# A float32 decoder trunk on one core: twelve instead of eight row tiles of each down projection as seven products, and more low parts of the mixers' weights made by transfers

## The chip, the core and the metric

The kernel runs on one core of a Trainium2 chip. Its time is the device time of one execution in microseconds (us), the median of several runs; lower is better. Four engines of the core work side by side, each through its own queue in order: PE (TensorE, matrix products), DVE (VectorE), ACT (ScalarE) and POOL (GpSimd, which here only issues transfers). SP issues the other transfers. Engines wait for one another by semaphores.

## The reference

Two layers; in each, a first feed-forward half step, a mixer (a gated recurrence beside windowed attention, joined through sigmoid gates) and a second feed-forward half step, each between two RMS norms. x is 512 tokens by 1024, all in float32. What the change touches:

```python
def swiglu(h, w_gate, w_up, w_down):              # D_MODEL = 1024, D_FF = 2816 = 22 * 128
    return (jax.nn.silu(h @ w_gate) * (h @ w_up)) @ w_down
...
    x = x + 0.5 * rms_norm(swiglu(h, w_ffn1_gate[l], w_ffn1_up[l], w_ffn1_down[l]), gn[1])
...
    mixed = jax.nn.sigmoid(gate_a) * y_hg + jax.nn.sigmoid(gate_b) * y_at
    x = x + rms_norm(mixed @ w_out[l], gn[3])
...
    x = x + 0.5 * rms_norm(swiglu(h, w_ffn2_gate[l], w_ffn2_up[l], w_ffn2_down[l]), gn[5])
```

The gates gate_a and gate_b are columns of h @ w_in[l]; y_hg and y_at are the two branches after their own projections.

## The kernel before

**Three matmuls for one.** A float32 operand is split into a high part (rounded to the fast matmul format) and the rest, its low part. `mm3` adds high x high, high x low and low x high, so one product of tiles is three matmuls. Of a weight tile, ACT makes the high part `whi` (a cast) and DVE the low part `wlo` (a subtraction). For tiles of kind v, a and d the low part is made otherwise: ACT writes the negated weights, rounded, to `wlo` (`scalar.mul(it.lo, w, -1.0)`), and a transfer issued by POOL adds the raw weights onto them (`accum_op=ALU.add`), so that the difference is left. Activations are split in the same way by ACT and DVE (both are called `s` in the profile, and every accumulator in PSUM is called `acc`).

**The weights' stream.** The class `Stream` (`ws`) loads all weights in order through SP: raw tiles `w` of 128x1024 into 5 buffers (`W32`), each freed when its last reader is done. `split` turns a raw tile, or a sum of raw tiles built by DVE in a buffer `tt` (of which there are 2), into a piece of `whi` and `wlo` in 6 buffers (`WS`). `ws.lead` says how many pieces are prepared ahead: 3, and 5 within a down projection. A piece's buffers come free when PE has used the piece six places earlier.

**Seven products.** A 2x2 block product takes seven products of quarter size instead of eight if sums and differences of the quarters are formed first (numbered 1 to 7 here, as in `operand`). The gate and up projections and a part of the mixers' gates are done so (`sevenths`, 256-column matmuls). Of a down projection, the row tiles in `SEVEN = (7, 11)`, counted in pairs, are: 8 of 22. Token halves and halves of the row tiles are the quarters of the activations, row halves and column halves (h = 0, 1) those of the weights.

**A down projection before** (`Down.seven`; four of them, two in each layer). Seven plain pieces for columns h = 0 (24 matmuls each, into four accumulators, one for each 128 tokens), then the seven products, each as two pieces of 12 matmuls in a row: 1, 5, 6, 2, 7, 4, 3. Then seven plain pieces for h = 1. Products 1, 6, 7 and 3 add up in the same two accumulators (token tiles 0 and 1), and `keep` has ACT copy them to SBUF between two products, because the other quarters need the partial sums: the copy after product 1 is s1, that after 6 is s2, that after 7 is s3. Product 6 adds onto the accumulators that s1 is copied from, so its first matmul waits for the copy. `sums`, `lower` and `differences` build the activations' operands: each takes DVE instructions of 256 columns, an ACT cast and a DVE subtraction of 512.

**The order of the work.** PE's order is the order in which the code is written, with `order.poll()` letting side work in. The other engines' queues are filled by a scheduler from the same program; on each of them an instruction that waits holds up all that stands behind it.

**The mixers.** `LATE = 6` of the 8 column tiles of the attention gate are plain projections (`branch`), the others, and all eight of the other gate, go in pairs as seven products (`branches`).

Of the kernel before, what the change touches and what calls it, by code (L numbers as in the profile page):

```python
# [7 lines left out]
F32 = mybir.dt.float32  # L8
# [3 lines left out]
ALU = mybir.AluOpType  # L12
# [3 lines left out]
P = 128  # L16
# [13 lines left out]
SLOTS = 59  # L30
SEVEN, LAST = (7, 11), 4
BANKS, RESERVE = 8, 2
# [9 lines left out]
def trunk(ctx: ExitStack, tc: tile.TileContext, xin, wall, gains, lbT, hgain, sinks, c_dist, c_mask, c_ident, out):  # L42
# [162 lines left out]
    class Item:  # L205


        def __init__(self, kind, u, left=8):
            self.kind, self.u, self.left = kind, u, left

    class Stream:
# [58 lines left out]
        def rows(self, kt, order=None):  # L270

            u0, r0 = self.n, self.n - self.off
            at = {p: i for i, p in enumerate(order or [(j, h) for j in range(kt // 2) for h in range(2)])}
            for j in range(kt // 2):
                for h in range(2):
                    b = [(4 * h + i) * kt + 2 * j for i in range(4)]
                    if kt == 8:
                        c = b[0] % 8 * P
                        self.src[u0 + at[j, h]] = [(None, wall[r0 + 4 * h : r0 + 4 * h + 4, :, c : c + 2 * P].rearrange("u p c -> p u c"))]
                    else:  # L280
                        self.src[u0 + at[j, h]] = [
                            (slice(i * 2 * P, (i + 1) * 2 * P), wall[r0 + n // 8][:, n % 8 * P : (n % 8 + 2) * P])
                            for i, n in enumerate(b)
                        ]
            if not order:
                self.plain(kt)

        def downs(self):

            a, b = SEVEN  # L290
            rest = [j for j in range(FT // 2) if not a <= j < b]
            m = (b - a) // 2
            up, low = range(a, a + m), range(a + m, b)
            first = [(j, 0) for j in rest]
            seven = [(j, h) for js, h in ((up, 0), (up, 1), (low, 1), (low, 0)) for j in js]
            self.rows(FT, first + seven + [(j, 1) for j in rest])
            self.plain(3, "v")
            self.plain(len(rest) - 3)
            u = self.n
            for kind, q in (("1", 0), ("5", 1), ("6", 2), ("7", 2), ("2", 3), ("4", 3), ("3", 2)):  # L300
                self.items += [Item(kind, u + m * q + i) for i in range(m)]
            self.n += 4 * m
            self.plain(len(rest))

# [18 lines left out]

        def sevens(self, it):

            u, m = it.u, (SEVEN[1] - SEVEN[0]) // 2
            w = self.raw[u]
            if it.kind == "5":
                t = self.tt[u] = sb.tile([P, D], F32, tag="tt", name=nm("tt"), bufs=2)
                vector.tensor_tensor(t, w, self.raw[u - m], op=ALU.subtract)  # L330
                self.release(u - m)
                return t
            if it.kind == "6":
                t = self.tt[u - m]
                vector.tensor_tensor(t, w, t, op=ALU.subtract)
                return t
            if it.kind == "7":
                t = self.raw[u - m]
                vector.tensor_tensor(t, w, t, op=ALU.subtract)
                return t  # L340
            if it.kind == "4":
                t = self.tt.pop(u - 2 * m)
                vector.tensor_tensor(t, w, t, op=ALU.subtract)
                return t
            return w

        def split(self):
            it = self.items[self.done]
            u, last = it.u, it.kind in "uvd"
            self.load(u + (1 if it.kind in "uv1234567" else 2))  # L350
            it.hi = sb.tile([P, D], F32R, tag="whi", name=nm("whi"), bufs=WS)
# [13 lines left out]
            elif it.kind == "c":  # L365

                t = sb.tile([P, D], F32, tag="tt", name=nm("tt"), bufs=2)
                vector.tensor_tensor(t[:, h[0]], self.t13[:, h[0]], v[:, h[1]], op=ALU.add)
                vector.tensor_tensor(t[:, h[1]], t[:, h[0]], w[:, h[1]], op=ALU.add)
                w = t  # L370
            elif it.kind == "d":
                w = v
                cols = h[1:]
            elif it.kind in "1234567":
                w = self.sevens(it)
# [10 lines left out]
            self.flight += 1  # L386
            m = (SEVEN[1] - SEVEN[0]) // 2
            if last:
                self.release(*range(u, u + (1 if it.kind in "uv" else 2)))
            elif it.kind == "7":  # L390
                self.release(u - m)
            elif it.kind in "43":
                self.release(u)

# [239 lines left out]
    class Down:  # L634
# [3 lines left out]
        def __init__(self, src, l, n, nxt):  # L638
# [5 lines left out]
            self.ss = [small([P, 2], "ss2", 8) for _ in range(TT)]  # L644
            self.left = TT

        def gain(self):
# [35 lines left out]
        def post(self, t):  # L683
            for h in range(2):
                if self.yg[t][h] is None:
                    self.square(t, h, self.y[t][h])
                    self.scaled(t, h, self.y[t][h])
            rc = self.root(self.ss[t])
# [120 lines left out]

        def product(self, n, bs, t0, h, start, stop):  # L810

            for u, b in enumerate(bs):
                for t in range(2):
                    for i in range(2):
                        st = cut(self.operand(n, 2 * u + i), slice(t * P, (t + 1) * P))
                        mv = [w.rearrange("p (m two c) -> p m two c", two=2, c=P)[:, :, i, :] for w in b[2:]]
                        mm3(self.y[t0 + t][h], st, mv, start and u == i == 0, stop and (u, i) == (len(bs) - 1, 1), True)
                        order.poll()
                    ws.used(b)

        def seven(self):
# [7 lines left out]
            for t in range(TT):  # L829
                y[t][0] = acc()  # L830
            work = [lambda q=q: self.raws(q) for q in range(m)] + [lambda p=p: self.sums(p) for p in range(2 * m)]
            work += [lambda p=p: self.lower(p) for p in range(m)]
            ws.lead = 5
            for n, j in enumerate(js):
                self.ready(ks[: 4 * n + 4 + EARLY])
                for w in work[2 * n - 2 : 2 * n] if n else ():
                    w()
                b = ws.next(8, TT)
                for t in range(TT):
                    for i in range(2):  # L840
                        self.piece(b, t, 0, j, i, n == i == 0, False, True)
                    ws.used(b)
                    order.poll()
            for t in range(TT):
                y[t][1] = acc()

            def take(n):
                return [ws.next(8, 2) for _ in range(n)]

# [5 lines left out]

            self.product(1, take(m), 0, 1, True, True)
            s1 = keep(0)
            for p in range(m):
                self.differences(p)
            self.product(5, take(m), 2, 1, True, True)  # L860
            s5 = keep(2)
            for p in range(m, 2 * m):
                self.differences(p)
            self.product(6, take(m), 0, 1, False, True)
            s2 = keep(0)
            b7 = take(m)
            self.product(2, take(m), 0, 0, False, True)
            for t in range(2):
                vector.tensor_tensor(s5[t], s5[t], s2[t], op=ALU.add)
            self.product(7, b7, 0, 1, False, True)  # L870
            s3 = keep(0)
            for t in range(2):
                vector.tensor_copy(y[t][1], s5[t])
                vector.tensor_tensor(y[2 + t][1], y[2 + t][1], s3[t], op=ALU.add)
            self.product(4, take(m), 2, 0, False, True)
            self.gain()
            self.product(3, take(m), 0, 1, False, False)
            self.residual()
# [6 lines left out]
            for j in js[: len(js) - LAST]:  # L885
                b = ws.next(8, TT)
                for t in (2, 3, 0, 1):
                    for i in range(2):
# [657 lines left out]
```

## Time and profile before

| | |
|---|---|
| median of three runs | 2093.43 us (2093.42 to 2093.84) |
| the profiled execution | 2094.18 us, span 2092.4 us, granted TensorE clock 0.999 |
| PE busy | 2085.2 us, 100% of the span, 13129 matmuls |
| DVE busy | 1583.7 us, 76% |
| ACT busy | 1191.5 us, 57% |
| DMA | 313.67 MB, mean 150 GB/s |
| low parts by transfer | 188 (105 of 512 KB, 83 of 256 KB) |

Busy times of different engines overlap. In the profile `L169` is the line of every matmul and `L162` that of every DVE and ACT instruction, so instructions are told apart by the names of their tiles. A start that is given as "D0 + n" below counts from the first matmul of a down projection.

### The profile page before, as it was taken

How to read it: one execution, taken by the hardware profiler on the slowest of the kernel's cores; microseconds unless marked ns; L12 is line 12 of the kernel's file. 1: busy time of each engine (PE TensorE's matmuls, PEld its weight loads, DVE VectorE, ACT ScalarE, POOL GpSimd, SP SyncE). 2: the span in 40 equal slices, each digit the busy share in tenths (PEclk: the TensorE clock that was granted, in tenths of full speed). 3: DMA queues.
4: the chain of work that ended last, by engine and by line, in shares of the span. 5: the costliest groups of instructions: out<-in, count | busy, mean ns of one | idle time of the engine just before them, and what ended most of it. 6: DMA issues, size and time to landing. Idle time of an engine off the chain costs nothing.

```text
span 2092.4 us, 34536 instructions
## 1 busy us (share of the span) xinstructions
PE 2085.2 (100%) x13129; PEld 1879.9 (90%) x13129; DVE 1583.7 (76%) x2768; ACT 1191.5 (57%) x1906; POOL 162.1 (8%) x192
## 2 busy tenths in 40 slices
PE   9999999999999999999999999999999999999999
PEld 7999988888898899998889998898788988999987
DVE  6987785777875688878488877758888748888693
ACT  7666655455554656665566665644565546566652
POOL 0111100000010011110001110000000000111100
PEclk9999999999999999999999999999999999999999
DMA  8588734222156758783666776532121666577732
GB/s 250 144 205 191 187 121 166 98 74 72 31 152 196 186 142 189 186 200 105 199 170 177 180 189 167 175 117 91 62 70 54 169 191 182 154 186 180 196 126 66
DMA packets 150918, 313.67 MB, mean 150 GB/s; under 512 B 16128, under 2 KB 73952, under 8 KB 150752
## 3 DMA queue, kind: packets, MB, share of 16 engines
q1 hardware_dynamic: 123536, 234.60, 34.0%
q0 software_dynamic: 27072, 76.82, 20.8%
q8 instruction: 103, 1.69, 0.3%
q14 instruction: 63, 0.52, 0.1%
q10 hardware_dynamic: 144, 0.05, 0.0%
HBM read 219.87 MB, written 14.73 MB: 112 GB/s over the span
## 4 chain that ended last, share of the span: by engine, by line
PE 99%; DMA 0%; DVE 0%; ACT 0%; SPq 0%; issue 0%
PE acc L169 97%; PE acc L177 2%; DMA s<-xin 0%; DVE wlo L162 0%; ACT whi L162 0%; DVE s L162 0%; ACT s L162 0%; SPq L314 0%; SPq L1398 0%; SPq L185 0%; DVE rt L162 0%
## 5 line engine op out<-in xcount | busy, mean ns | idle before, releaser
L169 PE MATMUL acc<-s,whi 128*128 128x256 f32 (+1 forms) x6152 | 1275.7, 306 | 0.0
L169 PEld LDWEIGHTS acc<-s,whi 128*128 128x128 f32 x6152 | 996.7, 191 | 47.9 <-issue 0.5
L169 PE MATMUL acc<-s,wlo 128*128 128x256 f32 (+1 forms) x3076 | 937.5, 305 | 0.6 <-DVE wlo L162 0.5
L169 PEld LDWEIGHTS acc<-s,wlo 128*128 128x128 f32 x3076 | 587.7, 191 | 26.5 <-DVE wlo L162 1.4
L169 PE MATMUL acc<-whi,s 128*128 128x512 f32 x1856 | 582.0, 391 | 0.0
L162 ACT CAST whi<-w 128x1024 fp32r<-128x1024 f32 (+1 forms) x373 | 354.5, 953 | 317.5 <-PE acc L169 174.4
L169 PEld LDWEIGHTS acc<-whi,s 128*128 128x128 f32 x1856 | 348.5, 188 | 75.1 <-issue 3.2
L169 PE MATMUL acc<-wlo,s 128*128 128x512 f32 x928 | 361.3, 389 | 0.0
L162 DVE TENSOR_TENSOR wlo<-w,whi 128x1024 fp32r<-128x1024 f32 (+1 forms) x185 | 223.9, 1215 | 117.2 <-ACT whi L162 107.5
L382 POOL DMA_DIRECT2D wlo<-w x188 | 161.9, 861 | 1802.3 <-ACT wlo L162 826.5
L162 ACT CAST whi<-tt 128x1024 fp32r<-128x1024 f32 x190 | 199.4, 1049 | 162.1 <-DVE tt L162 138.3
L162 DVE TENSOR_TENSOR s<-s,s 128x256 f32<-128x256 f32 (+4 forms) x481 | 246.8, 542 | 19.0 <-ACT s L162 15.8
L162 DVE TENSOR_TENSOR wlo<-tt,whi 128x1024 fp32r<-128x1024 f32 x190 | 231.9, 1220 | 17.7 <-ACT whi L162 15.7
L169 PEld LDWEIGHTS acc<-wlo,s 128*128 128x128 f32 x928 | 174.3, 188 | 34.9
L162 DVE TENSOR_TENSOR m<-acc,s 128x512 f32<-128x512 f32 (+1 forms) x249 | 145.1, 587 | 68.3 <-PE acc L169 65.2
L162 ACT ACTIVATE wlo<-w 128x1024 fp32r<-128x1024 f32 (+1 forms) x188 | 163.2, 868 | 18.3 <-PE acc L169 17.9
L162 ACT CAST s<-s 128x512 fp32r<-128x512 f32 (+1 forms) x180 | 97.1, 586 | 112.8 <-DVE s L162 112.7
L162 DVE TENSOR_TENSOR tt<-tt,w 128x512 f32<-128x512 f32 x166 | 114.6, 690 | 4.6
L162 ACT COPY s<-acc 128x512 f32<-128x512 f32 (+2 forms) x181 | 85.4, 484 | 54.1 <-PE acc L177 28.9
L162 ACT ACTIVATE s<-acc 128x512 f32<-128x512 f32 (+1 forms) x101 | 58.5, 600 | 68.3 <-PE acc L169 67.7
L162 DVE SCALAR_TENSOR_TENSOR s<-m 128x512 f32<-128x512 f32 x73 | 50.4, 691 | 50.7 <-ACT m L162 50.7
L162 ACT ACTIVATE s<-s 128x512 f32<-128x512 f32 (+1 forms) x86 | 53.7, 630 | 51.3 <-DVE s L162 51.2
(95 smaller groups left out, 1225.5 us busy)
## 6 DMA issues: line engine op xcount, KB each, us to landing
w<-wall SPq DMA_DIRECT2D x275, 512.0 KB, 3.9
wlo<-w POOLq DMA_DIRECT2D x105, 512.0 KB, 5.7
w<-wall SPq DMA_DIRECT2D x352, 128.0 KB, 2.9
wlo<-w POOLq DMA_DIRECT2D x83, 256.0 KB, 3.9
x_d<-s SPq DMA_DIRECT2D x48, 256.0 KB, 2.2
s<-x_d SPq DMA_DIRECT2D x48, 256.0 KB, 5.1
w<-wall SPq DMA_DIRECT2D x42, 256.0 KB, 3.1
grow<-rows_d SPq DMA_DIRECT2D x6, 512.0 KB, 4.3
```

The source lines that it names most:

```text
L162: return f(*a, **kw)
L169: nc.tensor.matmul(o, lhsT, rhs, start=start, stop=stop, skip_group_check=loose)
L177: nc.tensor.transpose(o, src, ident)
L382: nc.gpsimd.dma_start(it.lo[:, c].bitcast(F32), w[:, c], accum_op=ALU.add)
```

## The change

Down projections: `SEVEN` becomes (5, 11), so twelve row tiles (three groups of two upper and two lower tiles, called units here) go by seven products, and ten are plain. The order of the work is rewritten: four plain pieces for h = 0, the three pieces of product 1, then for each unit one piece each of products 5, 6, 4 and 2, then the three pieces of product 7, the fifth plain piece (`MID`), the three of product 3 and the plain pieces of h = 1. For a unit's sums of weights only one `tt` buffer is used, in place: raw tile minus raw tile gives 5, a third raw tile minus that gives 6, a fourth minus that gives 4. The raw tiles for 7 and 3 are loaded a second time, nine tiles more in each down projection. Kind "tv" (the plain pieces 0 to 2, the pieces of products 1 and 2) has its low part made by a transfer. The sum s5 + s2 is no longer written back into an accumulator but added in `post` (`also`).

Mixers: `LATE` becomes 4, so one more pair of gate tiles goes by seven products, and the low parts of 14 pieces of each mixer are made by transfers instead of by DVE.

```diff
-SEVEN, LAST = (7, 11), 4
+SEVEN, LAST, MID = (5, 11), 4, 1
-W32, WS, AHEAD, TAIL, PLAIN, FIRST, EARLY, LATE = 5, 6, 3, 2, 3, 6, 4, 6
+W32, WS, AHEAD, TAIL, PLAIN, FIRST, EARLY, LATE = 5, 6, 3, 2, 3, 6, 4, 4
...
+            def five(c, u):
+                c[0] = sb.tile([P, D], F32, tag="tt", name=nm("tt"), bufs=2)
+                sub(c[0], raw[u + 1], raw[u])
+                return c[0]
+
+            def onto(c, u):
+                sub(c[0], raw[u], c[0])
+                return c[0]
...
+            plain(min(3, len(front)), "tv")
+            plain(len(front) - 3, "t")
+            plain(m, "tv")
+            for _ in range(m):
+                u, c = self.n, [None]
+                item("t", u + 1, lambda c=c, u=u: five(c, u), (u, u + 1))
+                item("t", u + 2, lambda c=c, u=u: onto(c, u + 2), (u + 2,))
+                item("t", u + 3, lambda c=c, u=u: onto(c, u + 3))
+                item("tv", u + 3, lambda u=u: raw[u + 3], (u + 3,))
+                self.n += 4
...
-                if it.kind in "vad":
+                if it.kind in ("v", "a", "d", "tv"):
...
+            for u in range(m):
+                self.unit(1, u, 0, 1, True)
             s1 = keep(0)
...
+            for u in range(m):
+                for f, v in work[2 + 2 * u : 4 + 2 * u]:
+                    pair(f, v)
+                self.unit(5, u, 2, 1, True)
+                if u == m - 1:
+                    s5 = keep(2)
+                self.unit(6, u, 0, 1, False)
+                if u == m - 1:
+                    s2 = keep(0)
+                self.unit(4, u, 2, 0, False)
+                self.unit(2, u, 0, 0, False)
...
-                ws.plain(2 * H + 6 + 8 + LATE * 3 // 2)
+                ws.plain(2 * H + 6)
+                ws.plain(8 + LATE * 3 // 2, "v")
```

Three places of the first down projection, in the engines' own orders. The order is the same in the other three. First PE, where product 5 ends (accumulators 3248 and 3249 before, 3146 and 3147 now) and product 6 begins; before, with two pieces of product 5 between product 1 and here:

```order
L169 MATMUL acc_3249<-whi_3177,s_3106 128x512
L169 MATMUL acc_3249<-wlo_3178,s_3106 128x512
L169 MATMUL acc_3249<-whi_3177,s_3107 128x512
L169 MATMUL acc_3246<-whi_3212,s_3057 128x512
L169 MATMUL acc_3246<-wlo_3213,s_3057 128x512
```

And now:

```order
L169 MATMUL acc_3147<-whi_3043,s_3069 128x512
L169 MATMUL acc_3147<-wlo_3044,s_3069 128x512
L169 MATMUL acc_3147<-whi_3043,s_3070 128x512
L169 MATMUL acc_3144<-whi_3097,s_3062 128x512
L169 MATMUL acc_3144<-wlo_3098,s_3062 128x512
```

Product 6 of unit 0 now starts on product 1's accumulators (3144, 3145) one piece of 12 matmuls after product 1 has ended, where it was two pieces.

Second ACT, around the copies of product 1's accumulators (s1). Before:

```order
L162 CAST whi_3212<-tt_3136 128x1024
L162 CAST whi_3241<-tt_3179 128x1024
L162 CAST whi_3262<-w_523_2943 128x1024
L162 COPY s_3294<-acc_3246 128x512
L162 CAST whi_3284<-w_526_2952 128x1024
L162 COPY s_3295<-acc_3247 128x512
```

Now (s_3158 is the high part of the fourth sum of activations, which belongs to unit 1; s_3162 and s_3166 are parts for unit 1 too):

```order
L162 ACTIVATE wlo_3183<-w_526_2954 128x1024
L162 CAST whi_3182<-w_526_2954 128x1024
L162 CAST s_3158<-s_3155 128x512
L162 CAST s_3162<-s_2492 128x512
L162 CAST whi_3204<-tt_3206 128x1024
L162 CAST s_3166<-s_2625 128x512
L162 COPY s_3242<-acc_3144 128x512
L162 COPY s_3243<-acc_3145 128x512
```

The copies now stand behind four casts for unit 1, the first of which reads a sum that DVE makes.

Third DVE, where its work on the down projection begins, before:

```order
L162 SCALAR_TENSOR_TENSOR s_2912<-m_2761 128x512
L162 TENSOR_TENSOR s_2924<-s_646,s_2923 128x512
L162 TENSOR_TENSOR s_2928<-s_780,s_2927 128x512
L162 TENSOR_TENSOR s_2932<-s_917,s_2931 128x512
L162 TENSOR_TENSOR s_2936<-s_1052,s_2935 128x512
L162 TENSOR_TENSOR tt_3136<-w_523_2943,w_500_2861 128x1024
```

Now:

```order
L162 SCALAR_TENSOR_TENSOR s_2912<-m_2761 128x512
L162 TENSOR_TENSOR s_2924<-s_646,s_2923 128x512
L162 TENSOR_TENSOR s_2928<-s_780,s_2927 128x512
L162 TENSOR_TENSOR s_2932<-s_917,s_2931 128x512
L162 TENSOR_TENSOR tt_3045<-w_503_2884,w_500_2861 128x1024
L162 TENSOR_TENSOR s_2936<-s_1052,s_2935 128x512
```

The first subtraction of raw tiles (`tt`) stands one row earlier and reads raw tiles 7 and 8 of the down projection (w_500, w_503) instead of 7 and 9. From it to the instruction that completes s_3155, DVE's order now holds 35 instructions.

More of the change, by code (lines that the diff above doesn't have):

```diff
@@ L293, in downs @@
             up, low = range(a, a + m), range(a + m, b)
[L294 to L301, printed above, removed]
@@ L808, in operand, with unit @@
             return cut((self.x24 if n in (2, 4) else self.x37)[p], HALF[n in (3, 4)])
[L810 to L819, printed above, removed]
+        def unit(self, n, u, t0, h, start):
+            b = ws.next(8, 2)
+            for t in range(2):
+                for i in range(2):
+                    st = cut(self.operand(n, 2 * u + i), slice(t * P, (t + 1) * P))
+                    mv = [w.rearrange("p (m two c) -> p m two c", two=2, c=P)[:, :, i, :] for w in b[2:]]
+                    mm3(self.y[t0 + t][h], st, mv, start and u == i == 0, False, True)
+                    order.poll()
+                ws.used(b)
         def seven(self):
@@ L886, in seven @@
                 b = ws.next(8, TT)
-                for t in (2, 3, 0, 1):
+                for t in range(TT):
                     for i in range(2):
```

137 lines of the change are left out of this document (76 added, 61 removed).

## Prediction

> **What bounds the kernel now.** I read the busy times first, then the chain that ended last, then the stretches of one down projection.
>
> ```profile
> PE 2085.2 (100%) x13129; PEld 1879.9 (90%) x13129; DVE 1583.7 (76%) x2768; ACT 1191.5 (57%) x1906; POOL 162.1 (8%) x192
> PE 99%; DMA 0%; DVE 0%; ACT 0%; SPq 0%; issue 0%
> core 0: us, PE busy (x) PEld busy (x) DVE busy (x) ACT busy (x) POOL busy (x), PEclk, DMA share, GB/s
> 239.30:277.40 38.10, 38.10 (x170) 31.56 (x169) 31.27 (x49) 18.40 (x29) 0.00 (x0) 1.00 0.47 139
> 277.40:315.50 38.10, 38.10 (x169) 31.53 (x168) 32.00 (x38) 22.15 (x29) 0.00 (x0) 1.00 0.52 160
> ```
>
> PE is busy for 2085.2 of 2092.4 us, and the chain is PE from end to end. The two stretches are the plain pieces for h = 0 of the first down projection and its seven products: PE never waits there, and DVE has 6 to 7 us of air in each 38. So time can be won only by fewer or shorter matmuls, and lost by any wait of PE, of which there is now next to none.
>
> **What PE saves.** The pitch of matmuls, start to start, from PE's timeline: three matmuls of 512 columns, then three of 256.
>
> ```profile
> 241.16 0.61 PE L169 MATMUL acc<-whi,s 128*128 128x512 f32 x2
> 241.84 0.61 PE L169 MATMUL acc<-whi,s 128*128 128x512 f32 x2
> 238.24 0.40 PE L169 MATMUL acc<-s,whi 128*128 128x256 f32 x2
> 238.60 0.40 PE L169 MATMUL acc<-s,whi 128*128 128x256 f32 x2
> ```
>
> That is 0.68/3 = 0.2267 us and 0.36/3 = 0.12 us each. A down projection had 14 x 24 + 14 x 12 = 504 matmuls of 512 columns and now has 10 x 24 + 21 x 12 = 492: 12 x 0.2267 = 2.72 us, four times 10.88. In each mixer two plain gate tiles (48 matmuls of 512, 10.88 us) become seven products (84 of 256, 10.08 us): 0.80 each, 1.6 together. PE saves 12.5 us if it waits nowhere.
>
> **Where it will wait.** Product 6 of unit 0 needs s1 copied out of its accumulators first. PE reaches it after 4 x 24 + 3 x 12 + 12 = 144 matmuls, at D0 + 144 x 0.2267 = D0 + 32.64 us. ACT does the copies only after four casts, the first of which needs the sum s_3155 from DVE. So I count DVE's order from its first subtraction of raw tiles to s_3155: 8 instructions of 1024 columns, 8 of 512, 19 of 256. Their pitches, where DVE runs through (starts of neighbouring rows):
>
> ```profile
> 246.94 2.49 DVE L162 TENSOR_TENSOR s<-s,s 128x512 fp32r<-128x512 f32 x4
> 252.92 1.23 DVE L162 TENSOR_TENSOR tt<-w,w 128x1024 f32<-128x1024 f32 x1 [3.49 <-DMA w<-wall]
> 254.06 1.22 DVE L162 TENSOR_TENSOR wlo<-w,whi 128x1024 fp32r<-128x1024 f32 x1
> 255.20 0.69 DVE L162 TENSOR_TENSOR s<-s,s 128x512 fp32r<-128x512 f32 x1
> 255.80 1.22 DVE L162 TENSOR_TENSOR tt<-w,w 128x1024 f32<-128x1024 f32 x1
> 278.18 0.41 DVE L162 TENSOR_TENSOR s<-s 128x256 f32<-128x256 f32 x1
> 278.52 1.02 DVE L162 TENSOR_TENSOR s<-s,s 128x512 fp32r<-128x512 f32 x2
> ```
>
> 1.14, 0.60 and 0.34 us: 8 x 1.14 + 8 x 0.60 + 19 x 0.34 = 20.4 us. Then ACT, pitches again:
>
> ```profile
> 227.93 1.05 ACT L162 CAST whi<-w 128x1024 fp32r<-128x1024 f32 x1 [1.73 <-issue]
> 228.88 1.05 ACT L162 ACTIVATE wlo<-w 128x1024 fp32r<-128x1024 f32 x1
> 245.59 2.17 ACT L162 CAST s<-s 128x512 fp32r<-128x512 f32 x4
> 281.76 0.59 ACT L162 COPY s<-acc 128x512 f32<-128x512 f32 x1 [0.32 <-PE acc L169]
> ```
>
> Three casts of 512 columns (2.17/4 = 0.54 each), one of 1024 (0.95) and the copy (0.59): 3.2 us, with 0.1 for the hand-over to PE 3.3. If DVE's subtraction starts at D0 + t, PE waits t + 20.4 + 3.3 - 32.64 = t - 8.9 us. That ACT stands behind a late DVE is nothing strange here:
>
> ```profile
> ACT s L162 <- DVE s L162: 172.1, 94, 9.1
> ```
>
> **What t is.** The subtraction needs raw tile 8. These are PE's first rows of the four down projections (D0), and SP's last of four transfers for raw tile 8 in each, with the time to its landing:
>
> ```profile
> 239.32 0.40 PE L169 MATMUL acc<-whi,s 128*128 128x512 f32 x1
> 932.32 0.40 PE L169 MATMUL acc<-whi,s 128*128 128x512 f32 x1
> 1274.26 0.40 PE L169 MATMUL acc<-whi,s 128*128 128x512 f32 x1
> 1967.25 0.40 PE L169 MATMUL acc<-whi,s 128*128 128x512 f32 x1
> ...
> L311 SPq DMA_DIRECT2D w<-wall x1: 430/430/430, 246.3 to 246.3; - x1
> DMA to landing us min/median/max: 5.1/5.1/5.1
> L311 SPq DMA_DIRECT2D w<-wall x1: 437/437/437, 939.1 to 939.1; - x1
> DMA to landing us min/median/max: 3.8/3.8/3.8
> L311 SPq DMA_DIRECT2D w<-wall x1: 432/432/432, 1281.7 to 1281.7; - x1
> DMA to landing us min/median/max: 3.6/3.6/3.6
> L311 SPq DMA_DIRECT2D w<-wall x1: 430/430/430, 1975.1 to 1975.1; - x1
> DMA to landing us min/median/max: 3.3/3.3/3.3
> ```
>
> Landed at D0 + 12.1, 10.6, 11.0 and 11.1; the waits would be 3.2, 1.7, 2.1 and 2.2 us, 9.2 together. But now the low parts of product 1's pieces are transfers too, and two of them are issued before that landing, when ACT has raw tiles 4 and 5.
>
> ```profile
> q0 software_dynamic: 27072, 76.82, 20.8%
> wlo<-w POOLq DMA_DIRECT2D x105, 512.0 KB, 5.7
> L311 SPq DMA_DIRECT2D w<-wall x1: 1302/1302/1302, 236.4 to 236.4; - x1
> DMA to landing us min/median/max: 7.1/7.1/7.1
> ```
>
> The queue q0 carries these transfers: 20.8% of 2092.4 us is 435 us for 76.8 MB, so 512 KB take about 3 us of all 16 engines. The last two rows show a load of raw tile 5 that lies between two of them: issue held up to 1.3 us, landing after 7.1. Against the 3.3 to 5.1 above that is 2 to 4 us more. Raw tile 9 no longer crowds raw tile 8 (SP now holds its load until the transfer from raw tile 4 is done), which gives back about 1. I take 2 us, with 0 and 4 as ends. The four waits are then 5.2, 3.7, 4.1 and 4.2: 17.2 us.
>
> **The rest of the change.**
> - SP loads nine raw tiles more in each down projection, and loads wait for low-part transfers. Behind the held load of tile 9, tiles 10 to 12 take four issues of 0.43 us each (the rows above), 1.7; tile 12 is needed 9.5 us after the first subtraction by the pitches above. Cost 0; if DVE does catch up with it, the lateness adds to each wait, up to 2 us. POOL's queue holds nothing but such transfers.
> - Product 2 of unit 1 has its low part by transfer, behind an ACT cast that waits for DVE. By the same counting its matmuls would wait 0.6 us less than product 6 did, so they fall into the wait already paid. Products 4 and 2 of unit 2 likewise, by under 1 us. I add nothing; a transfer slower than 5.7 would be paid in full.
> - DVE's load within the products falls (over the kernel 56 subtractions of 1024 columns from raw tiles fewer, 32 on sums of tiles more), but only behind the place where PE waits.
> - The additional sum in `post` (0.60 us of DVE) lies under the next token tile's matmuls, 24 x 0.2267 = 5.4 us.
> - The mixers' 28 additional transfers free DVE of 28 x 1.14 us and cost ACT a pass each. A piece there lasts 5.4 us, three are made ahead, the transfer takes 5.7: hidden. PE's whole idle time before was 2092.4 - 2085.2 = 7.2 us, start and end included, so there is little to win. 0, within 1 us for each mixer.
>
> **Sum.** -10.9 - 1.6 + 17.2 = +4.7 us on the profiled 2094.18 us; that run lies 0.75 above the median of 2093.43, so 2098.2 on the median's scale.
>
> **Rivals.**
> - *DVE keeps ahead of the loads* (faster). If raw tile 8 were no limit, DVE would arrive at the subtraction about D0 + 10: before, its four activation rows (the row at 246.94) ended at D0 + 10.1; one of them now stands behind the subtraction, and a pass more of ACT ahead of them. Each wait is then 1.1 us: -12.5 + 4.4 = -8.1, 2085. Against it speaks that the landings above are all later. It decides below a mean wait of 2.1 us.
> - *The landings stay as they are*: -12.5 + 9.2 = -3.3, 2090. The loads of tile 8 stand ahead of most of the second transfer; the row with 7.1 us speaks against.
> - *The clock falls during the waits.* The only stretch of several us in which PE idles is the end:
>
> ```profile
> 2084.00:2088.00 4.00, 3.64 (x28) 2.97 (x26) 2.67 (x6) 1.56 (x4) 0.00 (x0) 1.00 0.35 101
> 2088.00:2092.40 4.40, 0.01 (x1) 0.00 (x0) 0.06 (x1) 0.38 (x2) 0.00 (x0) 0.71 0.42 119
> ```
>
> The granted clock (third number from the right) is 0.71 there. If matmuls ran at 0.71 after each wait for as long as it lasted, 4.3 x (1/0.71 - 1) = 1.8 us, four times 7: 2105. [...] The row of the end agrees that idling lowers the clock, but nothing here shows whether a wait of 4 us is enough.
>
> **How the numbers follow.** About 0.2% (4.2 us) is what a measurement can tell from no change. Forecast, waits with landings 1 to 4 us later: 2094 to 2106, likeliest 2098, chance 0.42. Landings as before, 2087 to 2094: 0.25. DVE ahead, 2081 to 2087: 0.20. Clock: 0.13, 2102 to 2109. Slower: the clock and 0.32 of the forecast, 0.45. Faster: DVE ahead and 0.07 of the second, 0.27. Within 0.2%: 0.28. The range 2084 to 2106 leaves out some 0.1 at each end.
>
> **What would show it.** PE should show one wait for ACT of 2 to 6 us at D0 + 32.6 in each down projection, ended by the copy `s<-acc`; DVE no idle time from D0 + 13 to there; 12 matmuls less in each down projection at the same pitch; and the page 244 low-part transfers instead of 188. The forecast is wrong if PE's chain is still unbroken there (then DVE had its tile earlier), or if PE waits at products 4 or 2 instead, or in the mixers.

## The result, and the profile after

The changed kernel takes 2119.5 us (median of four runs, 2117.2 to 2122.3) against 2093.6 us (the three runs of before and a fourth, 2094.00): 1.0124 times the time before, 95% interval 1.0112 to 1.0136. The sign was forecast; the size was not (2098.2 us, range to 2106). The profiled run has a span of 2116.7 us against 2092.4, 24.3 us more. The page of the changed kernel, its busy times, queues, chain, one group of matmuls and the low-part transfers:

```profile
PE 2084.8 (98%) x13153; PEld 1880.8 (89%) x13153; DVE 1587.9 (75%) x2808; ACT 1256.2 (59%) x1994; POOL 210.2 (10%) x248
...
q1 hardware_dynamic: 144848, 253.48, 36.1%
q0 software_dynamic: 35136, 105.66, 28.1%
...
PE 86%; DMA 5%; issue 4%; SPq 2%; ACT 1%; DVE 1%; POOL 0%; POOLq 0%; DVEq 0%; ACTq 0%
...
wlo<-w POOLq DMA_DIRECT2D x159, 512.0 KB, 5.6
...
wlo<-w POOLq DMA_DIRECT2D x85, 256.0 KB, 3.8
```

The chain of work that ended last has left PE: 14% of it now runs through transfers, issue, ACT and DVE. The low parts made by transfers are 159 + 85 = 244, as the change says. PE's waits (total, times, longest), and from the timeline the four places (start, duration, and in brackets the idle time before it and who ended it):

```profile
PE acc L169 <- ACT s L162: 25.9, 4, 6.6
```

```profile
277.73 0.80 PE L169 MATMUL acc<-whi,s 128*128 128x512 f32 x1 [6.39 <-ACT s L162]
278.32 0.63 PE L169 MATMUL acc<-wlo,s 128*128 128x512 f32 x1
278.75 1.05 PE L169 MATMUL acc<-whi,s 128*128 128x512 f32 x2
...
977.04 0.80 PE L169 MATMUL acc<-whi,s 128*128 128x512 f32 x1 [6.65 <-ACT s L162]
...
1325.63 0.80 PE L169 MATMUL acc<-whi,s 128*128 128x512 f32 x1 [6.38 <-ACT s L162]
...
2024.36 0.80 PE L169 MATMUL acc<-whi,s 128*128 128x512 f32 x1 [6.51 <-ACT s L162]
```

There is one wait in each down projection, at the first matmul of product 6 of unit 0, ended by ACT. ACT's timeline before the first of them shows the queue in front of the copy:

```profile
274.59 1.14 ACT L162 CAST s<-s 128x512 fp32r<-128x512 f32 x2 [1.70 <-DVE s L162]
275.63 1.04 ACT L162 CAST whi<-tt 128x1024 fp32r<-128x1024 f32 x1
276.58 0.61 ACT L162 CAST s<-s 128x512 fp32r<-128x512 f32 x1
277.10 1.06 ACT L162 COPY s<-acc 128x512 f32<-128x512 f32 x2
```

ACT stood idle until DVE gave it the first of four casts; the copies of product 1's accumulators, which had been ready for over 8 us, came behind them. DVE in turn had started on the units with this subtraction (the rows of the four down projections):

```profile
253.94 1.23 DVE L162 TENSOR_TENSOR tt<-w,w 128x1024 f32<-128x1024 f32 x1 [5.52 <-DMA w<-wall]
...
953.03 1.22 DVE L162 TENSOR_TENSOR tt<-w,w 128x1024 f32<-128x1024 f32 x1 [5.80 <-DMA w<-wall]
...
1301.85 1.23 DVE L162 TENSOR_TENSOR tt<-w,w 128x1024 f32<-128x1024 f32 x1 [4.52 <-DMA w<-wall]
...
2000.48 1.23 DVE L162 TENSOR_TENSOR tt<-w,w 128x1024 f32<-128x1024 f32 x1 [5.08 <-DMA w<-wall]
```

The first matmuls of the four down projections start at 238.48, 936.86, 1286.23 and 1984.78, so DVE began at D0 + 15.5, 16.2, 15.6 and 15.7, each time after waiting about 5 us for the load of raw tile 8. Finally the stretches of the first wait, of the piece behind it and of the next (length, busy us and instructions of each engine, then the granted clock, the DMA engines' share and GB/s):

```profile
271.30:277.70 6.40, 0.03 (x1) 0.00 (x0) 6.39 (x11) 4.70 (x8) 0.86 (x1) 0.85 0.65 136
277.70:282.80 5.10, 5.07 (x12) 4.01 (x13) 5.03 (x9) 2.02 (x3) 0.00 (x0) 0.52 0.87 253
282.80:285.60 2.80, 2.80 (x14) 2.28 (x14) 1.74 (x3) 1.31 (x2) 0.00 (x0) 1.00 0.63 188
```

Behind the wait the granted clock is 0.52, and twelve matmuls take 5.1 us (starts 0.43 us apart in the rows above) instead of 2.7. In the other three down projections they took 5.1 to 5.3 us, and in the fourth two matmuls behind them were slow as well, so that the slow clock cost 2.4, 2.6, 2.4 and 2.9 us. So the sum of the traces is -12.5 (matmuls) + 26.3 (waits in this group, 0.4 of them for DVE) + 10.3 (slow clock) = +24.1, within a microsecond of the 24.3 us.

### The profile page after: what moved, and what is told of

Its sections match the earlier page's. It is cut to its first block, busy times and chain, and to the rows that moved or that the text cites. A ratio compares the mean times of both kernels' runs of the same rounds, so it can differ in the third digit from the quotient of the medians.

```text
span 2116.7 us, 35203 instructions
## 1 busy us (share of the span) xinstructions
PE 2084.8 (98%) x13153; PEld 1880.8 (89%) x13153; DVE 1587.9 (75%) x2808; ACT 1256.2 (59%) x1994; POOL 210.2 (10%) x248
## 3 DMA queue, kind: packets, MB, share of 16 engines
HBM read 238.74 MB, written 14.73 MB: 120 GB/s over the span
## 4 chain that ended last, share of the span: by engine, by line
PE 86%; DMA 5%; issue 4%; SPq 2%; ACT 1%; DVE 1%; POOL 0%; POOLq 0%; DVEq 0%; ACTq 0%
PE acc L169 84%; DMA w<-wall 4%; SPq L356 2%; PE acc L177 2%; DMA wlo<-w 1%; DVE s L162 1%; ACT s L162 1%; DVE tt L162 0%; ACT wlo L162 0%; ACT whi L162 0%; POOL wlo L404 0%; ACT m L162 0%; DVE m L162 0%; POOLq L404 0%; DVEq L162 0%
## 5 line engine op out<-in xcount | busy, mean ns | idle before, releaser
L169 PEld LDWEIGHTS acc<-s,wlo 128*128 128x128 f32 x3100 | 592.4, 191 | 24.3 <-DVE wlo L162 0.3
L169 PE MATMUL acc<-whi,s 128*128 128x512 f32 x1824 | 580.7, 396 | 26.3 <-ACT s L162 25.9
L404 POOL DMA_DIRECT2D wlo<-w x244 | 210.0, 861 | 1837.7 <-ACT wlo L162 1086.4
L162 ACT CAST whi<-tt 128x1024 fp32r<-128x1024 f32 x206 | 216.1, 1049 | 224.3 <-DVE tt L162 203.6
L162 DVE TENSOR_TENSOR s<-s,s 128x256 f32<-128x256 f32 (+4 forms) x521 | 264.9, 538 | 22.3 <-ACT s L162 15.4
L162 DVE TENSOR_TENSOR wlo<-tt,whi 128x1024 fp32r<-128x1024 f32 x206 | 251.5, 1221 | 25.0 <-ACT whi L162 23.0
L162 ACT ACTIVATE wlo<-w 128x1024 fp32r<-128x1024 f32 (+1 forms) x244 | 221.9, 909 | 17.1 <-PE acc L169 16.7
L162 DVE TENSOR_TENSOR wlo<-w,whi 128x1024 fp32r<-128x1024 f32 (+1 forms) x129 | 154.2, 1212 | 60.5 <-ACT whi L162 58.6
L162 ACT CAST s<-s 128x512 fp32r<-128x512 f32 (+1 forms) x196 | 105.2, 579 | 83.6 <-DVE s L162 77.0
L162 ACT COPY s<-acc 128x512 f32<-128x512 f32 (+3 forms) x183 | 84.2, 486 | 30.1 <-PE acc L177 20.4
L162 DVE TENSOR_TENSOR tt<-w,w 128x512 f32<-128x512 f32 (+1 forms) x97 | 72.8, 750 | 21.1 <-DMA w<-wall 20.9
```

The lines of the kernel that those rows point to most:

```text
L162: return f(*a, **kw)
L169: nc.tensor.matmul(o, lhsT, rhs, start=start, stop=stop, skip_group_check=loose)
L404: nc.gpsimd.dma_start(it.lo[:, c].bitcast(F32), w[:, c], accum_op=ALU.add)
```

## The experiments

Each kernel was timed in three rounds or more beside the kernel before on the same chip. Ratios are to it, with 95% intervals.

| run | what it is | us | ratio |
|---|---|---|---|
| fill | changed + PE kept busy in the wait | 2116.8 | 1.0111 (1.0096 to 1.0126) |
| no_wait | changed, copy s1 not waited for | 2122.1 | 1.0134 (1.0119 to 1.0149) |
| m1_dve | changed, product 1's low parts by DVE | 2106.7 | 1.0065 (1.0049 to 1.0082) |
| mid_early | changed, fifth plain piece ahead of the units | 2139.3 | 1.0217 (1.0202 to 1.0233) |
| down_only | changed down projections alone | 2124.3 | 1.0145 (1.0129 to 1.0160) |
| mix_only | changed mixers alone | 2091.7 | 0.9991 (0.9981 to 1.0000) |
| both | m1_dve and mid_early | 2127.7 | 1.0165 (1.0148 to 1.0182) |
| trio | both, a piece moved behind product 7 | 2128.2 | 1.0163 (1.0148 to 1.0178) |
| m1_w6 | m1_dve, six raw buffers | 2117.3 | 1.0114 (1.0099 to 1.0129) |
| after_w6 | changed, six raw buffers | 2122.0 | 1.0137 (1.0121 to 1.0152) |
| both_w6 | both, six raw buffers | 2107.2 | 1.0064 (1.0049 to 1.0079) |
| mix2 | mix_only, one pair more | 2106.1 | 1.0059 (1.0042 to 1.0076) |
| m1_w6_nw | m1_w6, copy s1 not waited for | 2100.9 | 1.0037 (1.0024 to 1.0050) |
| both_w6_dve | both_w6, product 2's low parts by DVE | 2099.3 | 1.0027 (1.0017 to 1.0037) |

**fill: is it idleness that slows the matmuls?**

```diff
+                if u == 0:
+                    t = order.t
+                    for _ in range(14):
+                        mm(y[2][0][:, :P], zeros, ones, False, False, True)
+                    order.t = t
                 self.unit(6, u, 0, 1, False)
```

> The changed kernel, with 14 matmuls by a tile of zeros (128 columns each, some 0.45 us) put on PE in each down projection between product 5 and product 6 of unit 0, so that PE works through the wait for the copy instead of standing idle. The work of ACT, DVE and the queues is the same. My theory: the slow matmuls after the wait (pitch 0.427 us instead of 0.2267, granted clock 0.50) come from the idleness alone. Then the clock stays at 1.00 and product 6 takes 2.7 us instead of 5.1: 2.4 us less in each, 10 in all. But the pieces behind it were ready only 0.4 to 1.0 us before PE came to them (product 4 of unit 2 by DVE, product 2 of unit 2 by transfer, product 7's last piece by DVE), so I expect new waits there that take most of it: 2 us faster than the changed kernel, 2117, at best 2109. Rival: the matmuls are slow for another reason (the load on memory at that time); then the pitch stays 0.427 in that piece and the time within 1 us of the changed kernel.

The piece behind the first wait, and PE's waits in this run:

```profile
271.30:277.10 5.80, 3.32 (x29) 3.10 (x27) 5.79 (x11) 4.11 (x8) 0.86 (x1) 1.00 0.71 146
277.10:279.80 2.70, 2.66 (x11) 2.18 (x12) 2.67 (x5) 1.09 (x2) 0.00 (x0) 1.00 0.90 241
```

```profile
PE acc L169 <- ACT s L162: 12.7, 4, 3.9
PE acc L169 <- DMA wlo<-w: 4.2, 2, 3.2
...
PE acc L169 <- DVE wlo L162: 1.0, 2, 0.6
```

With the wait partly filled (the 14 matmuls took 3.29 us, 0.24 each and not the 0.45 expected) the clock stays at 1.00 and the twelve matmuls take 2.7 us: the slow clock comes from the idleness (in one of the four down projections 3.9 us of idleness were left, and there the clock fell to 0.50). The time is only 2.7 us below the changed kernel's, whose own runs spread over 5 us, because pieces behind are soon late themselves: 5.2 us of new waits for transfers and for DVE. Up to product 6 ACT and DVE work in the changed kernel's order here; behind it some of their rows have changed places, so these new waits need not all come from PE's being earlier.

**no_wait: is it the copy's place?** The place is changed so that nothing waits for the copy there:

```diff
-                self.unit(6, u, 0, 1, False)
+                self.unit(6, u, 0 if u else 2, 1, False)
```

> The changed kernel with product 6 of unit 0 added onto the accumulators of product 5 instead of those of product 1: the sums come out otherwise, the instructions on every engine and their order stay, and PE no longer has to wait for the copy s1 there. Theory A: the copy's place in ACT's queue is what costs the time; then the four waits (26 us) and the slow clock after them (10 us) go, and the kernel takes 2083. Theory B, mine now: from the first subtraction at D0 + 15.4 on DVE is the bound of the units, and the copy only showed it first. Without the copy PE waits later, in smaller pieces: by the rows of after at product 2 of unit 0 for its transfer (1.4 us), at product 4 of unit 1 for DVE (2.4), at product 2 of unit 1 for its transfer (2.6), at product 4 or 2 of unit 2 (2.3): about 8.7 us in each, no longer than 6.4 plus the 2.4 of the slow clock. Then 2117, and the granted clock near 1.00 if waits of 1 to 3 us don't lower it.

2122.1 us: nothing was won. ACT, DVE and POOL work in the same order as in the changed kernel. PE's waits in this run:

```profile
PE acc L169 <- DMA wlo<-w: 13.2, 6, 5.9
PE acc L169 <- DVE wlo L162: 11.1, 5, 3.6
PE acc L169 <- DVE s L162: 1.6, 1, 1.6
```

They add up to 25.9 us, as much as the waits at the copy did. The clock fell to 0.50 five times behind them, which theory B had left out; its time was 5 us too low. Theory A fell: in the changed kernel the copy is only the first to be late, and behind it the units' pieces by DVE and by transfer are late enough to take its place.

**m1_dve: do the transfers delay raw tile 8?**

```diff
-            plain(m, "tv")
+            plain(m, "t")
```

> The changed kernel with the low parts of product 1's three pieces made by DVE instead of by transfers. My theory: those transfers delay the landing of raw tile 8, at which DVE's first subtraction of the units starts (D0 + 15.4). Without them it lands about where it did in the kernel before, D0 + 11 to 12; DVE has 3.4 us more to do, but it stood idle for 4.5 to 5.8 us there. The wait at product 6 of unit 0 falls from 6.5 to about 2.6 us, the clock stays higher after it: 4 times 2.6 - 12.5 = -2 against before, 2092, and 2095 if the clock still falls. Rival: the landing is late because of the nine raw tiles more or the queue's order and not the transfers; then t stays at D0 + 15 and the time at 2119, or above it by DVE's 3.4 us.

The first subtraction in the first down projection (which starts at 238.70), and PE's waits:

```profile
249.78 1.23 DVE L162 TENSOR_TENSOR tt<-w,w 128x1024 f32<-128x1024 f32 x1 [2.24 <-DMA w<-wall]
```

```profile
PE acc L169 <- ACT s L162: 16.6, 8, 3.4
```

D0 + 11.1 instead of 15.5, so the three low-part transfers had cost 4.4 us of landing (4.0 to 5.2 in the four down projections): shown. The last of the four transfers for raw tile 8 was issued at D0 + 6.8 here and took 4.2 us to land; in the changed kernel it was issued at D0 + 9.6 and took 5.8. So most of the delay, 2.8 us, is that SP's issues ahead of it were held up, several by about a microsecond each. The first waits were 2.7 to 3.4 us, as expected. The time, 2106.7, was missed by 12 to 15 us: a second wait of 0.4 to 1.7 us came in each down projection, because a cast that waits for DVE now stands between the two copies, and in two of the four the clock fell to 0.50 all the same.

**mid_early, both and trio: more matmuls ahead of the units.**

```diff
-            order = [(j, 0) for j in front] + [(j, 0) for j in up]
+            order = [(j, 0) for j in front] + [(j, 0) for j in up] + [(j, 0) for j in mid]
...
+            plain(MID, "t")
...
-            plain(MID, "t")
...
             s1 = keep(0)
+            for n, j in enumerate(js[front:]):
+                plain(front + n, j)
...
-            for n, j in enumerate(js[front:]):
-                plain(front + n, j)
```

> The changed kernel with the fifth plain piece of h = 0 run between product 1 and unit 0 instead of between products 7 and 3. PE gets 5.44 us of matmuls ahead of the units, so each of their pieces is due 5.44 us later; DVE's first subtraction now takes raw tile 9, whose load is held by the low-part transfers, so it may start 1 to 3 us later. Product 3 loses the piece that lay between it and the copy s3 (about 1 us of wait). My theory (DVE's start and its work set when the units can go): the wait at product 6 of unit 0 becomes 1 to 4 us, the clock falls less or not at all: 4 times (1 to 4, + 1) - 12.5 = -4 to +7 against before, 2089 to 2101, likeliest 2094. Rival (the copy's place in the order is the cause, whatever DVE does): PE still waits 6 us there, 2115 to 2120.

A miss, 2139.3. The row of the first subtraction, which now needs raw tile 9, and the waits:

```profile
258.91 1.23 DVE L162 TENSOR_TENSOR tt<-w,w 128x1024 f32<-128x1024 f32 x1 [6.49 <-DMA w<-wall]
```

```profile
PE acc L169 <- ACT s L162: 33.2, 12, 5.5
```

It starts at 238.74, so this is D0 + 20.2: nearly five us later than for tile 8, not one to three. The 5.44 us that the piece gave were eaten by the load; the waits at product 6 are 4.0 to 5.5 us, and in each down projection a wait of 2.6 to 3.1 us came before product 3. The clock fell seven times instead of four (0.989 over the run, 0.992 in the changed kernel). Only with product 1's transfers gone too should the piece help:

> The changed kernel with two edits: the low parts of product 1 by DVE, and the fifth plain piece run between product 1 and unit 0. In the run with the second edit alone raw tile 9 landed at D0 + 20.4, five us later than tile 8 had, which ate the 5.4 us that the piece gave. My theory: without the low-part transfers tile 9 lands near D0 + 13 to 14 (tile 8 did at 11.2 in the run with the first edit alone), so the wait at product 6 of unit 0 falls to 0 to 1 us; what stays is the wait before product 3 for the copy s3 (3 us, ACT's queue holds it behind casts that wait for loads): 4 times (0.5 + 3) - 12.5 = +1.5, 2095, within 2090 to 2100. Rival: the loads, not the transfers, are the limit; tile 9 lands past D0 + 17, the wait stays above 3 us and the time above 2105.

The landing came as expected (251.94, D0 + 13.2), and the first waits fell to 1.0 to 2.5 us. But PE's waits were:

```profile
PE acc L169 <- ACT s L162: 17.5, 10, 2.9
PE acc L169 <- DMA wlo<-w: 11.2, 4, 5.0
PE acc L169 <- DVE wlo L162: 3.1, 4, 1.6
```

2127.7, a miss: 11.2 us for the low-part transfers of product 2, which I had not counted, and up to 2.9 us before product 3. Covering the latter with a piece of product 2 moved behind product 7 (`trio`) moved the wait, too:

> As the one with two edits, and product 2 of unit 2 run by PE behind product 7 (its piece is made at the old place), so that 2.7 us of matmuls lie between product 7 and product 3 and cover the copy s3. My theory: the wait before product 3 falls from about 3 to under 0.5 us; a new one of up to 1 us may come between products 6 and 7 for the copy s2, with product 4 of unit 2 to cover it. 4 times 1 - 12.5 = -8.5 at best, 2085; likeliest 2087. Rival: PE waits at the loads of products 7 and 3 whatever the order; then no faster than the kernel with two edits.

2128.2: the waits for copies fell from 17.5 to 7.7 us, and 17.0 us of waits for ACT's cast of product 7's weights came instead, one of 3.1 to 6.4 us in each down projection. In the first ACT itself had stood idle for 7.7 us until the load landed. The rival was right. Each repair brings forward the next piece that is late.

**Six raw buffers.**

```diff
-W32, ... = 5, ...
+W32, ... = 6, ...
-SLOTS = 59
+SLOTS = 57
```

> The changed kernel with six raw buffers instead of five, and two activation buffers less. Theory (buffers): the first subtraction moves from D0 + 15.4 to 12 to 14, the waits from 6.5 to 3 to 5 us; the clock still falls: 2105 to 2115. Rival (transfers and loads share what the DMA engines give, 0.95 of their time in that stretch): no earlier landing, 2119.

> The changed kernel with the low parts of product 1 by DVE, six raw buffers instead of five, and two of the 59 buffers for activations given up for it. Theory (raw tile 8 comes late because its buffer comes free late): its load starts a tile earlier, the first subtraction moves from D0 + 11.2 to 8.5 to 10, and the wait at product 6 of unit 0 from 2.7 to 3.4 us (with five buffers) to 0.5 to 2, short enough for the clock. 2095, within 2090 to 2100; the two activation buffers may cost 2 us. Rival (the loads themselves take the time, at 254 GB/s in that stretch): the subtraction stays at D0 + 11 and the time at 2106.

> The kernel with two edits (product 1's low parts by DVE, the fifth plain piece ahead of the units) with six raw buffers and two activation buffers less. With five, PE waited 0.4 to 5 us in each down projection for the low-part transfer of product 2 and 2.2 to 2.9 for the copy s3, behind casts that wait for loads. Theory (the loads of the units, 18 raw tiles and three transfers in 41 us of matmuls, are late because only five buffers take them): those waits shrink, 2105 to 2115. Rival (order on ACT and DVE): same, 2128.

In after_w6 (2122.0, neither theory) the subtraction moved to D0 + 13.5, but it now stands ahead of activation rows in DVE's queue, so DVE waited 12 us there and PE for DVE, already in the third plain piece, ahead of product 1:

```profile
252.36 1.23 DVE L162 TENSOR_TENSOR tt<-w,w 128x1024 f32<-128x1024 f32 x1 [12.04 <-DMA w<-wall]
```

```profile
254.84 1.06 PE L169 MATMUL acc<-whi,s 128*128 128x512 f32 x2 [4.46 <-DVE s L162]
```

In m1_w6 (2117.3) the subtraction came at D0 + 8.0, as early as expected, and yet PE waited 5.7 to 8.5 us at the copy: ACT's order had changed, and the copies stood behind more casts, which come later in DVE's order. Taking that wait away tells which it was:

> The kernel with six raw buffers and product 1's low parts by DVE, and product 6 of unit 0 added onto product 5's accumulators, so that PE doesn't wait there for the copy s1 (the sums come out otherwise). Theory: with the raw tiles landing early DVE has its pieces for the units ready in time, and the 26.7 us of waits at the copy, with the slow clock behind them (about 10 us), come from the copy's place behind casts that wait for DVE; without the wait the kernel is 25 to 35 us faster than with it, 2083 to 2092. Rival (DVE's own time is still the bound, as with five buffers): new waits of about the same sum, 2110 to 2120.

2100.9, between the two: 16.4 us came back. Here the copy's place does cost, about half; the rest returned mainly as 13.2 us of waits for product 2's transfers. both_w6 (2107.2) came out as the buffers' theory had it, 20.5 us below both, though no faster than m1_dve with five buffers; in m1_w6 and after_w6 the sixth buffer won nothing, so the buffers alone are not the limit. What was left in both_w6 were 9.5 us for transfers and 9.4 for copies, and with product 2's low parts by DVE:

```diff
-                item("tv", u + 3, lambda u=u: raw[u + 3], (u + 3,))
+                item("t", u + 3, lambda u=u: raw[u + 3], (u + 3,))
```

> The kernel with two edits and six raw buffers, and product 2's low parts by DVE too, so that no low part within the products is made by transfer. Theory (the transfers, issued only when ACT has written the negated weights and 5.7 us long, are late by themselves): the 9.5 us of waits for them and the slow clock after the longest (2.5 us) go, and DVE's 3 x 1.14 us more in each down projection cost up to half of that: 2095 to 2101. Rival (DVE sets the pace): each us more on DVE comes back as waits, 2107 or more.

2099.3, as expected; no wait for a transfer is left:

```profile
PE acc L169 <- ACT s L162: 10.4, 8, 2.5
PE acc L169 <- DVE wlo L162: 2.5, 4, 1.1
```

The clock is 1.000 in the profiled run. It is the best version with twelve tiles, 20.2 us faster than the changed kernel and still 0.27% slower than before. The sum fits less well here: -12.5 + 13.2 would be +0.7, the span is +4.6. The idle times are too small a measure of these waits, as the starts of the matmuls show:

```profile
2043.25 0.50 PE L169 MATMUL acc<-whi,s 128*128 128x512 f32 x1 [2.17 <-ACT s L162]
```

The matmul ahead of this one started at 2040.69, 2.56 us earlier; less one pitch of 0.23 that is 2.33 us lost, not 2.17, and the next start comes 0.34 us later instead of 0.23. So each wait cost some 0.27 us more than its idle time. The last down projection, from its first matmul to its last, took 118.1 us against 116.7 before; with its three waits counted in this way (3.9 us instead of 3.1) the twelve matmuls less gave 2.6 us of the 2.7 forecast, and in the other three down projections as much. Over the kernel the waits come to 16.2 us instead of 13.2, and 0.9 us of the span stay open.

**The parts apart.** `down_only` keeps `LATE = 6` and the mixers' plain pieces of before; `mix_only` is the kernel before with the other part:

```diff
-EARLY, LATE = ..., 6
+EARLY, LATE = ..., 4
...
-                ws.plain(2 * H + 6 + 8 + LATE * 3 // 2)
+                ws.plain(2 * H + 6)
+                ws.plain(8 + LATE * 3 // 2, "v")
```

> The changed kernel's down projections with the mixers of the kernel before (six plain attention-gate tiles, their low parts by DVE). My theory: all of the loss lies in the four down projections, the mixers give 1.6 us: 2121. Rival: the mixers' 28 further transfers cost time too (PE's other idle time, or loads that come late into the next down projection); then this kernel is faster than the changed one, by up to the 26 + 10 - 12.5 - 24.3 that the sum leaves open, about 1 us.

> The kernel before with the mixers' part of the change alone (four plain attention-gate tiles instead of six, 14 low parts of each mixer by transfers). My theory: 1.6 us faster than before by the six or so matmuls' worth of PE work, 2092.0, with 1 us either way. Rival: the additional transfers delay a load or a piece and PE waits in the mixers: 2094 or more.

The loss lies in the down projections: 2124.3 with them alone (2121.1 to 2126.0). That is 4.8 us above the changed kernel where 1.6 were expected; this run's profile has some 5 us of small waits for DVE and ACT in the down projections that the changed kernel's has not, and runs of both spread over 5 us. The mixers alone took 2091.7 (2091.3 to 2092.0 in ten runs; before 2093.4 to 2094.1 in thirteen): 1.9 us faster than before, 1.6 expected. It beats both kernels: the interval of its ratio only just reaches 1.0000, but none of its ten runs is as long as the shortest of before. Its chain and its waits:

```profile
PE 100%; DVE 0%; issue 0%; ACT 0%
```

```profile
PE acc L169 <- DVE eps_t L162: 1.1, 1, 1.1
PE acc L177 <- DVE s L162: 0.3, 1, 0.3
```

PE is unbroken from start to end, so here fewer matmuls are less time. From the first matmul of the first down projection to that of the second (with one mixer between) it took 692.1 us, before 693.0: 0.9 us for each mixer. One step more:

> The kernel before with the mixers' part of the change and one step more of it: two plain attention-gate tiles instead of four (LATE = 2). The mixers' part alone gave 1.9 us for one pair more in each of two mixers. Theory: another pair gives the same again, 2090. Rival: the sums for the seven products, which DVE now makes in two tiles' time instead of four, come late and PE waits: 2092 or more.

2106.1, the rival: in each mixer one wait of 4.37 us, of transposes for ACT, whose queue holds two pairs of casts there that wait for DVE; by their shapes DVE's rows there are the sums that are now made in half the time (read from the timeline, not tested). The clock falls behind both (0.996 over the run).

## Why the prediction was right or wrong

- **The mechanism** was right: one wait in each down projection, at product 6 of unit 0, ended by the copies s1, which stand behind four casts that wait for DVE; and t - 8.9 gives it: 6.6, 7.3, 6.7 and 6.8 us by the starts above, 6.4, 6.65, 6.4 and 6.5 measured (in the second 0.4 us of wait for DVE lies ahead of it).
- **The landing of raw tile 8 was mis-sized.** I took 2 us of delay by the low-part transfers, with 0 and 4 as ends. The subtractions began 3.4 to 5.6 us later than raw tile 8 had landed before, beyond my upper end in three of the four; m1_dve showed that product 1's transfers were the cause (D0 + 11.1 without). The row for it was in hand, a load of 7.1 us between two transfers, and I took the middle between the ends; I also counted the lateness of one load alone, where most of the delay had added up in the issues ahead of it. The waits were 25.9 us instead of 17.2: 8.7 of the 21 us by which the forecast fell short.
- **The clock was put among the rivals with 0.13 and is in the sum.** It fell to 0.50 in all four down projections and cost 2.4 to 2.9 us each, 10.3 us in all, on top of the waits; my estimate for it (1.8 us, from a clock of 0.71 at the kernel's end) was too low as well, since 0.71 was the mean over a stretch of 4.4 us. Every wait of PE of 3.9 us or more that the timelines of the runs show was followed by matmuls at the slow clock (last section), and the waits that came were 6.4 to 6.65 us. Once the waits were forecast at some 4 us, the two cases were not rivals but one. These two terms make 19.0 of the 21.3 us; the rest are small differences between the runs compared and 0.4 us of wait for DVE.
- **The matmuls saved**: the mixers' 1.6 us were 1.9, shown. The down projections' 10.9 could not be seen alone; the sum of the changed kernel closes with it within a microsecond, and in both_w6_dve, with the waits counted from start to start, 2.6 of 2.7 us a down projection show.
- **What was costed at nothing**: in the changed kernel the low parts of product 4 of unit 2, of product 2 of units 1 and 2 and of product 7's last piece were ready only 0.4 to 2.6 us before PE came to them, and that behind the wait and the slow clock. fill and no_wait came to them sooner and had new waits of 5 and 26 us. The prediction had product 2 only 0.6 us behind product 6; that was the sign that the copy is not the bound but the first of several things that are late.
- **"DVE keeps ahead"** (2085) was not reached by any rearrangement: the nearest, both_w6_dve, lies 6 us above before.

## What to carry to other kernels

When PE is unbroken, a saving of matmuls is worth its time only where the operands keep up: twelve matmuls less in a stretch that asks for more loads, more sums and later copies turned 2.7 us of gain into 6 to 7 us of loss, while the same kind of saving in a stretch with slack (the mixers) came through whole. When a wait is found, look how far behind it the next pieces are; if they are nearly as late, removing that wait may gain nothing (no_wait) or half of it (m1_w6_nw). In these runs a wait of PE of 3.9 us or more had the slow clock after it each time (2.4 to 2.9 us in the changed kernel), and one of 2.0 to 3.5 us some of the times; so a wait of some 4 us is to be priced with it, and a shorter one with a chance of it.

## What the runs showed of the hardware

The granted clock behind a wait was 0.50 in these traces, not a value between (by stretches of 1 us), and matmuls of 512 columns then started 0.43 us apart. It stayed there 6.8 us in the first three down projections of the changed kernel, 10.2 in the fourth, and 3.4 behind one wait of m1_dve: two, three and one times 3.4. In the fourth down projection PE fell idle at 2017.85, and the clock fell after 2.2 us of it (the wait up to there, the rest of it, the slow matmuls, the next ones):

```profile
2017.80:2019.90 2.10, 0.05 (x1) 0.00 (x0) 2.10 (x4) 1.77 (x2) 0.86 (x1) 1.00 0.02 4
2019.90:2024.30 4.40, 0.00 (x0) 0.00 (x0) 4.39 (x8) 3.08 (x6) 0.00 (x0) 0.51 0.90 191
2024.30:2030.20 5.90, 5.84 (x14) 4.59 (x15) 5.83 (x10) 2.15 (x4) 0.00 (x0) 0.50 0.85 253
2030.20:2032.00 1.80, 1.80 (x10) 1.49 (x9) 0.97 (x2) 1.08 (x2) 0.00 (x0) 0.98 0.51 167
```

In the other three it fell after 4.5, 5.2 and 4.5 us of idle time. In m1_dve a wait of 2.7 us was enough in the second down projection, and one of 3.4 us was not in the third (in both the wait first):

```profile
966.10:968.80 2.70, 0.00 (x0) 0.00 (x0) 2.70 (x6) 2.67 (x5) 0.00 (x0) 1.00 1.03 198
968.80:972.10 3.30, 2.58 (x6) 1.53 (x6) 3.30 (x6) 1.53 (x2) 0.00 (x0) 0.57 0.85 263
```

```profile
1312.10:1315.50 3.40, 0.03 (x1) 0.00 (x0) 3.40 (x8) 3.08 (x5) 0.00 (x0) 1.00 1.01 191
1315.50:1318.00 2.50, 1.65 (x6) 1.05 (x6) 2.50 (x4) 0.72 (x1) 0.00 (x0) 1.00 0.76 226
```

So the length of a wait alone did not decide. The starts of the slow stretches in the changed kernel are 275.82, 975.55, 1323.71 and 2020.03, which lie 205, 102 and 204 times 3.413 us apart; the two in m1_dve, 969.26 and 2010.32, lie 305 times as much apart. An estimate from these starts: counted on from the first of them in steps of 3.413 us, the wait of 3.4 us in m1_dve has 1.88 us of idle time in one step and 1.75 in the next (0.2 of it in the wait behind), and the wait of 2.7 us lies within one. That this is what decides was not tested.

By length, the waits that the timelines of the runs show came out like this: those of 1.0 to 1.94 us (the longest in both_w6) had matmuls at the full clock behind them, those of 3.86 us (m1_w6_nw) and more had slow ones each time, and between them both happened: slow behind 2.07 (m1_w6_nw) and 2.22 (both_w6), at full clock behind 2.51 (both_w6_dve) and 3.42 (m1_dve).
